# Sliding windows on one core: channel halves on partition halves, and output rows of 16 KB

## The chip, the cores and the metric

The kernel runs on one core of one Trainium2 chip. The metric is device time in microseconds for one execution, as the median of several.

## The reference

The input x holds 16 images of 64 channels, 64 x 64 float32 values each (16.8 MB). Windows of 8 x 8 are cut with a stride of 4 in both directions, 15 x 15 of them, and all are written out (59.0 MB). No arithmetic is done on the values.

```
n_h = (h - window_size) // stride + 1          # 15
n_w = (w - window_size) // stride + 1          # 15
result = np.zeros((batch, n_h, n_w, c, window_size, window_size), dtype=np.float32)
for i in range(n_h):
    for j in range(n_w):
        result[:, i, j] = x[:, :, i*stride : i*stride + window_size, j*stride : j*stride + window_size]
```

For one image and one window (i, j) the output is one contiguous run of 64 x 8 x 8 values, 16 KB.

## The kernel before

**Layout.** The whole input stays in SBUF in the tile L: 128 partitions, each with 32 channels of 16 image rows of 64 values (128 KB). A partition is an image (16), a channel half (2) and a quarter of the image's height (4), in this order, so that partition p is 8 x image + 4 x half + quarter. Within a quarter there are four window rows, numbered by the slot s = 0 to 3. Slot 3 needs the first four image rows of the next quarter, which lie on the next partition; the last quarter has no slot 3.

**Loads (L52).** Sixteen DMAs of 1 MB, eight issued from SP and eight from ACT, each with 32 partitions and 8 channels in runs of 4 KB.

**Index tiles (L62 to L78).** POOL writes the partition number, and DVE makes from it the output row at which each partition's store begins. In idx_last and idx_hlast the last quarter's rows are put out of range, and the scatter skips them.

**A window (L112 to L125).** One pass of the function window makes column j and slot s for all images and quarters at once, in a buffer of the tiles G. For slots 0 to 2 it is one ACT copy (L112). For slot 3 it is a DVE copy of the upper four rows (L114) and a DVE shuffle that brings the lower four from the next partition (L115). Then POOL issues an indirect DMA (L125), called scatter here, which writes one row of 8 KB for each partition, since a partition has half the channels. There are nine buffers of 1 MB. A copy into a buffer waits until the store that read it last has landed.

**Order.** For the first 8 windows the first 16 channels of each half are done first, with rows of 4 KB, because the load brings these channels earlier. The other halves of these windows alternate with whole windows, two and two. The last two windows are stored by seven plain DMAs from SP (L119), each for one quarter. Column by column, slots 0 to 3 follow each other. The engines' instructions are put in order by the framework, which also sets the waits; SP, ACT and POOL each have a DMA queue of their own, and all three use the same 16 DMA engines.

Of the kernel before, what the change touches and what calls it, by code (L numbers as in the profile page):

```python
# [1 line left out]

# [4 lines left out]


@with_exitstack  # L10
def kernel(
    ctx: ExitStack,
    tc: tile.TileContext,
    x: bass.AP,
    window_size: int,
    stride: int,
    out: bass.AP,
):
    nc = tc.nc
    P = nc.NUM_PARTITIONS  # L20

    B, C, H, W = x.shape
    Bo, NH, NW, Co, WSo, WSo2 = out.shape
    WS = int(window_size)
    ST = int(stride)
    assert Bo == B and Co == C and WSo == WS and WSo2 == WS

    f32 = mybir.dt.float32
    i32 = mybir.dt.int32
    ALU = mybir.AluOpType  # L30
    HQ = 4
    CH = P // (B * HQ)
    CL = C // CH
    RB = H // HQ
    NSLOT = RB // ST
    NWIN = NH * NW
    CFREE = CL * WS * WS
    assert HQ == 4 and CH == 2 and WS == 2 * ST

    lpool = ctx.enter_context(tc.tile_pool(name="lpool", bufs=1))  # L40
    ipool = ctx.enter_context(tc.tile_pool(name="ipool", bufs=1))
    gpool = ctx.enter_context(tc.tile_pool(name="gpool", bufs=1))


    L = lpool.tile([P, CL, RB, W], f32)
    x_v = x.rearrange("b (ch cl) (hq r) w -> hq (b ch) cl (r w)", ch=CH, hq=HQ)
    NCH = 4
    cw = CL // NCH

    for k in (2, 0, 1, 3):  # L50
        for q in range(HQ):
            (nc.sync, nc.scalar)[q % 2].dma_start(  # L52
                out=L[q::HQ, k * cw : (k + 1) * cw, :, :],
                in_=x_v[q, :, k * cw : (k + 1) * cw, :],
            )


    def itile(name):
        return ipool.tile([P, 1], i32, name=name)

    pi, tb, tq, tc_, idx, idx_last = (itile(n) for n in ("pi", "tb", "tq", "tc", "idx", "idx_last"))
    nc.gpsimd.iota(pi[:, :], pattern=[[0, 1]], base=0, channel_multiplier=1)  # L62
    nc.vector.tensor_scalar(out=tb[:, :], in0=pi[:, :], scalar1=3, scalar2=None, op0=ALU.logical_shift_right)  # L63
    nc.vector.tensor_scalar(out=tc_[:, :], in0=pi[:, :], scalar1=2, scalar2=1, op0=ALU.logical_shift_right, op1=ALU.bitwise_and)  # L64
    nc.vector.tensor_scalar(out=tq[:, :], in0=pi[:, :], scalar1=HQ - 1, scalar2=None, op0=ALU.bitwise_and)  # L65
    nc.vector.tensor_scalar(out=tb[:, :], in0=tb[:, :], scalar1=float(NWIN * CH), scalar2=None, op0=ALU.mult)  # L66
    nc.vector.tensor_tensor(out=tb[:, :], in0=tb[:, :], in1=tc_[:, :], op=ALU.add)  # L67
    nc.vector.tensor_scalar(out=tc_[:, :], in0=tq[:, :], scalar1=float(NSLOT * NW * CH), scalar2=None, op0=ALU.mult)  # L68
    nc.vector.tensor_tensor(out=idx[:, :], in0=tb[:, :], in1=tc_[:, :], op=ALU.add)  # L69

    nc.vector.tensor_scalar(out=tq[:, :], in0=tq[:, :], scalar1=float(HQ - 1), scalar2=float(2 * B * NWIN * CH), op0=ALU.is_equal, op1=ALU.mult)  # L71
    nc.vector.tensor_tensor(out=idx_last[:, :], in0=idx[:, :], in1=tq[:, :], op=ALU.add)  # L72


    HCL = CL // 2
    idx_h, idx_hlast = itile("idx_h"), itile("idx_hlast")
    for d, e in ((idx_h, idx), (idx_hlast, idx_last)):
        nc.vector.tensor_scalar(out=d[:, :], in0=e[:, :], scalar1=2.0, scalar2=None, op0=ALU.mult)  # L78
    o_v = out.rearrange("b i j (ch cl) r w -> (b i j ch) (cl r w)", ch=CH)
    o_h = out.rearrange("b i j (ch cl) r w -> (b i j ch) (cl r w)", ch=2 * CH)  # L80
    nxt = [min(p + 1, 31) for p in range(32)]

    order = [(j, s) for j in range(NW) for s in range(NSLOT)]


    TAIL, BACK = 2, 3
    o_q = out.rearrange("b i j (ch cl) r w -> i j b ch (cl r w)", ch=CH)

    def free(st):
        tc.declare_no_dep(st.ins, group="stores", reason="each store writes rows of its own")  # L90
        tc.add_to_no_dep_group("stores", st.ins)


    UNITS = 18
    G = [gpool.tile([P, 2 * HCL, WS, WS], f32, name=f"G{n}") for n in range(UNITS // 2)]
    at = 0

    def window(j, s, half):
        nonlocal at
        cols = slice(j * ST, j * ST + WS)  # L100
        last = s == NSLOT - 1
        if half is None:
            n, c0 = 2, 0
            at += at % 2
        else:
            n, c0 = 1, half * HCL
        u = at % UNITS
        at += n
        cs = slice(c0, c0 + n * HCL)
        g = G[u // 2][:, u % 2 * HCL : (u % 2 + n) * HCL, :, :]  # L110
        if not last:
            nc.scalar.copy(out=g, in_=L[:, cs, s * ST : s * ST + WS, cols])  # L112
        else:
            nc.vector.tensor_copy(out=g[:, :, 0:ST, :], in_=L[:, cs, s * ST : RB, cols])  # L114
            nc.vector.stream_shuffle(out=g[:, :, ST:WS, :], in_=L[:, cs, 0:ST, cols], mask=nxt)  # L115
        if (j, s) in order[-TAIL:]:
            g_q = g.rearrange("(m q) c r w -> q m (c r w)", q=HQ)
            for q in range(HQ - 1 if last else HQ):
                free(nc.sync.dma_start(out=o_q[q * NSLOT + s, j], in_=g_q[q]))  # L119
            return  # L120
        if half is None:
            o, ix = o_v, (idx_last if last else idx)
        else:
            o, ix = o_h, (idx_hlast if last else idx_h)
        st = nc.gpsimd.indirect_dma_start(  # L125
            out=o,
            out_offset=bass.IndirectOffsetOnAxis(ap=ix[:, 0:1], axis=0),
            in_=g.rearrange("p c r w -> p (c r w)"),
            in_offset=None,
            element_offset=(s * NW + j) * CH * CFREE + (half or 0) * HCL * WS * WS,  # L130
            bounds_check=B * NWIN * CH * (1 if half is None else 2) - 1,
            oob_is_err=False,
        )
        free(st)

    EARLY = 8
    for j, s in order[:EARLY]:
        window(j, s, 0)
    late = list(order[:EARLY])
    rest = list(order[EARLY:])  # L140
    while late:
        for w in late[:2]:
            window(*w, 1)
        for w in rest[:2]:
            window(*w, None)
        late, rest = late[2:], rest[2:]
    for w in rest[:-TAIL]:
        window(*w, None)
    at -= 2 * BACK
    for w in rest[-TAIL:]:  # L150
        window(*w, None)


# [1 line left out]
_INS = ['x', 'window_size', 'stride']  # L155
_OUTS = [((16, 15, 15, 64, 8, 8), 'float32')]

_NUMBERS = {'window_size': 8, 'stride': 4}


# [26 lines left out]
```

## Time and profile before

| what | value |
|---|---|
| median of 11 runs | 193.7 us (192.97 to 194.13) |
| profiled execution | 193.53 us, span 191.8 us |
| DVE busy | 30.2 us, 16% of the span |
| ACT busy | 86.2 us, 45% |
| POOL busy | 64.4 us, 34% |
| DMA | 75.80 MB, 395 GB/s on average |

Busy times are sums over the span of the profiled execution. POOL's busy time is nearly all from issuing scatters, 0.97 us each; the bytes move later, on the DMA engines. In a row of waits the numbers are the sum in us, how often, and the longest. In a group of instructions they are the busy time, the mean in ns, and the idle time of the engine just before, with what ended it. The 40 slices of the page are 4.8 us long each.

### The profile page before, as it was taken

The page shows a single profiled execution, that of the slowest core. Times are in us where ns is not written, and L with a number is a line of the kernel's source. Part 1 is how long each engine was busy: PE and PEld are TensorE (multiplying, and loading weights), DVE is VectorE, ACT ScalarE, POOL GpSimd, SP SyncE. Part 2 cuts the span into 40 slices and gives each one's busy share as a digit, 9 for nine tenths or more (in the row PEclk, how much of TensorE's full clock was granted, in tenths as well). Part 3 has the DMA queues.
Part 4 walks back from the last instruction along what each step waited for, and adds up shares of the span by engine and source line. Part 5 has one row for each costly group of instructions (what it writes and reads, how often), then busy time and mean ns, then how long its engine had stood idle before and what let it go on. Part 6 is the DMA issues. An engine that isn't in the chain of part 4 may idle for free.

```text
span 191.8 us, 458 instructions
## 1 busy us (share of the span) xinstructions
DVE 30.2 (16%) x62; ACT 86.2 (45%) x52; POOL 64.4 (34%) x71
## 2 busy tenths in 40 slices
DVE  2000000402322121211203120303030303000030
ACT  0000000494999646565655656474747373300300
POOL 0000000177877763543434344444444444400000
DMA  5999999999999999999999999999999999999785
GB/s 173 422 412 410 408 410 410 410 410 418 420 430 416 424 420 407 414 415 417 408 419 417 415 403 408 414 410 408 410 405 408 412 407 412 405 410 427 309 272 185
DMA packets 14196, 75.80 MB, mean 395 GB/s; under 512 B 1936, under 2 KB 1936, under 8 KB 7952
## 3 DMA queue, kind: packets, MB, share of 16 engines
q0 software_dynamic: 9504, 57.15, 73.1%
q1 hardware_dynamic: 2512, 10.22, 13.8%
q10 hardware_dynamic: 2176, 8.39, 11.1%
q14 instruction: 4, 0.03, 0.0%
HBM read 16.78 MB, written 62.65 MB: 414 GB/s over the span
## 4 chain that ended last, share of the span: by engine, by line
DMA 66%; issue 26%; POOL 3%; DVE 1%; POOLq 0%; DVEq 0%; PEldq 0%
DMA out_dram<-G,idx 57%; DMA out_dram<-G,idx_last 5%; DMA out_dram<-G,idx_h 4%; POOL out_dram L125 3%; DVE G L115 1%; DVE G L114 0%; POOLq L125 0%; POOL pi L62 0%; DVEq L114 0%; PEldq L182 0%
## 5 line engine op out<-in xcount | busy, mean ns | idle before, releaser
L112 ACT COPY G<-L 128x2048 f32<-128x2048 f32 (+1 forms) x51 | 84.9, 1696 | 59.3 <-DMA out_dram<-G,idx_last 25.0
L125 POOL DMA_INDIRECT out_dram<-G,idx x38 | 36.8, 969 | 49.6 <-DMA out_dram<-G,idx 46.4
L114 DVE COPY G<-L 128x1024 f32<-128x1024 f32 (+1 forms) x17 | 10.9, 638 | 152.9 <-DMA out_dram<-G,idx 88.5
L115 DVE STREAM_SHUFFLE G<-L 128x1024 f32<-128x1024 f32 (+1 forms) x17 | 19.5, 1146 | 0.0
L112 ACT ACT_TABLE_LOAD x1 | 1.3, 1283 | 36.2 <-DMA L<-in_x_dram 36.2
L125 POOL DMA_INDIRECT out_dram<-G,idx_hlast x4 | 4.0, 1004 | 37.6 <-DVE G L115 36.7
L125 POOL DMA_INDIRECT out_dram<-G,idx_last x12 | 11.6, 963 | 11.7 <-DVE G L115 7.8
L125 POOL DMA_INDIRECT out_dram<-G,idx_h x12 | 11.7, 975 | 3.7 <-issue 2.4
L63 DVE TENSOR_SCALAR tb<-pi 128x1 int32<-128x1 int32 x1 | 0.2, 153 | 1.0 <-POOL pi L62 1.0
L62 POOL IOTA pi<- 128x1 int32 x1 | 0.1, 121 | 0.4 <-PEq L182 0.4
L115 DVE LOAD_MASK_SELECT G<-L x17 | 0.2, 13 | 0.0
L168 POOL MEMSET const-float32-0.0<- 128x1 f32 x1 | 0.1, 99 | 0.2 <-issue 0.2
L69 DVE CUSTOM_DVE_ANT_0 idx<-tb,tc 128x2 uint16<-128x2 uint16 x1 | 0.2, 160 | 0.0
L67 DVE CUSTOM_DVE_ANT_0 tb<-tb,tc 128x2 uint16<-128x2 uint16 x1 | 0.2, 159 | 0.0
L78 DVE TENSOR_SCALAR idx_hlast<-idx_last 128x1 int32<-128x1 int32 x1 | 0.2, 155 | 0.0
L68 DVE TENSOR_SCALAR tc<-tq 128x1 int32<-128x1 int32 x1 | 0.2, 154 | 0.0
L78 DVE TENSOR_SCALAR idx_h<-idx 128x1 int32<-128x1 int32 x1 | 0.2, 154 | 0.0
L72 DVE CUSTOM_DVE_ANT_0 idx_last<-idx,tq 128x2 uint16<-128x2 uint16 x1 | 0.2, 153 | 0.0
L66 DVE TENSOR_SCALAR tb<-tb 128x1 int32<-128x1 int32 x1 | 0.1, 148 | 0.0
L71 DVE TENSOR_SCALAR tq<-tq 128x1 int32<-128x1 int32 x1 | 0.1, 147 | 0.0
L64 DVE TENSOR_SCALAR tc<-pi 128x1 int32<-128x1 int32 x1 | 0.1, 144 | 0.0
L65 DVE TENSOR_SCALAR tq<-pi 128x1 int32<-128x1 int32 x1 | 0.1, 143 | 0.0
(3 smaller groups left out, 0.3 us busy)
## 6 DMA issues: line engine op xcount, KB each, us to landing
L<-in_x_dram ACTq DMA_DIRECT2D x8, 1024.0 KB, 19.8
L<-in_x_dram SPq DMA_DIRECT2D x8, 1024.0 KB, 20.1
out_dram<-G SPq DMA_DIRECT2D x7, 256.0 KB, 4.2
out_dram<-G,idx POOLq DMA_INDIRECT x38, 18.7
out_dram<-G,idx_h POOLq DMA_INDIRECT x12, 7.0
out_dram<-G,idx_last POOLq DMA_INDIRECT x12, 18.8
out_dram<-G,idx_hlast POOLq DMA_INDIRECT x4, 8.0
```

Of the source, the lines that this page charges most:

```text
L62: nc.gpsimd.iota(pi[:, :], pattern=[[0, 1]], base=0, channel_multiplier=1)
L63: nc.vector.tensor_scalar(out=tb[:, :], in0=pi[:, :], scalar1=3, scalar2=None, op0=ALU.logical_shift_right)
L64: nc.vector.tensor_scalar(out=tc_[:, :], in0=pi[:, :], scalar1=2, scalar2=1, op0=ALU.logical_shift_right, op1=ALU.bitwise_and)
L67: nc.vector.tensor_tensor(out=tb[:, :], in0=tb[:, :], in1=tc_[:, :], op=ALU.add)
L68: nc.vector.tensor_scalar(out=tc_[:, :], in0=tq[:, :], scalar1=float(NSLOT * NW * CH), scalar2=None, op0=ALU.mult)
L69: nc.vector.tensor_tensor(out=idx[:, :], in0=tb[:, :], in1=tc_[:, :], op=ALU.add)
L72: nc.vector.tensor_tensor(out=idx_last[:, :], in0=idx[:, :], in1=tq[:, :], op=ALU.add)
L78: nc.vector.tensor_scalar(out=d[:, :], in0=e[:, :], scalar1=2.0, scalar2=None, op0=ALU.mult)
L112: nc.scalar.copy(out=g, in_=L[:, cs, s * ST : s * ST + WS, cols])
L114: nc.vector.tensor_copy(out=g[:, :, 0:ST, :], in_=L[:, cs, s * ST : RB, cols])
L115: nc.vector.stream_shuffle(out=g[:, :, ST:WS, :], in_=L[:, cs, 0:ST, cols], mask=nxt)
L125: st = nc.gpsimd.indirect_dma_start(out=o, out_offset=bass.IndirectOffsetOnAxis(ap=ix[:, 0:1], axis=0), in_=g.rearrange("p c r w -> p (c r ...
```

## The change

A partition now is a channel half (2), an image (16) and a quarter (4), in this order, so that partitions 0 to 63 hold channels 0 to 31 and partitions 64 to 127 hold channels 32 to 63. A buffer of G is 128 partitions with all 64 channels, 16 KB each, 2 MB together, and there are four. One buffer holds two slots: partitions 0 to 63 one, partitions 64 to 127 the other. Since the channels of a window lie on both halves of L, each half of a buffer is filled by two copies (by two copies and two shuffles for slot 3): one from its own partitions, one from the other 64.

The 24 loads take 8 partitions each. The images come in two groups of eight (y = 0, 1). For each group and quarter SP loads 28 channels of half 0, and POOL the other 4 channels of half 0 and then all 32 of half 1. ACT issues no loads. The index tiles are made ahead of the loads, by 21 DVE instructions in place of 11.

For the first three columns, slots 0 and 1 are done by image group, six units of 1 MB. In their scatters the rows of the other group are skipped; the buffer partitions that these skipped rows would read are filled with zeros by DVE first, eight fills. After that come 27 units of two slots each. Slots 0 and 1 take ACT for the copies on the same partitions and DVE for the shifted ones. Slots 2 and 3 take ACT for both copies of slot 2 and DVE for slot 3; which half of the buffer holds slot 3 alternates with the column. The last unit is slots 0 and 1 of the last column, stored by eight DMAs from SP, each with 16 rows of 16 KB.

The core of the diff:

```
-    HQ = 4
-    CH = P // (B * HQ)
+    CH = 2
+    HQ = P // (B * CH)
...
-    for k in (2, 0, 1, 3):
-        for q in range(HQ):
-            (nc.sync, nc.scalar)[q % 2].dma_start(
-                out=L[q::HQ, k * cw : (k + 1) * cw, :, :],
-                in_=x_v[q, :, k * cw : (k + 1) * cw, :],
-            )
+    x_v = x.rearrange("(y b) (ch cl) (hq r) w -> ch y hq b cl (r w)", y=NY, ch=CH, hq=HQ)
+    SMALL = 4
+    def load(eng, ch, y, q, c0, c1):
+        p0 = ch * HP + y * QP + q
+        eng.dma_start(out=L[p0 : p0 + QP - HQ + 1 : HQ, c0:c1, :, :], in_=x_v[ch, y, q, :, c0:c1, :])
...
+    for y in range(NY):
+        for q in range(HQ):
+            load(nc.sync, 0, y, q, SMALL, CL)
+            load(nc.gpsimd, 0, y, q, 0, SMALL)
+            load(nc.gpsimd, 1, y, q, 0, CL)
...
+    NG = 4
+    G = [gpool.tile([P, C, WS, WS], f32, name=f"G{n}") for n in range(NG)]
...
+    def fill(g, half, s, j, lo, n, copies):
+        d = slice(half * HP + lo, half * HP + lo + n)
+        cols = slice(j * ST, j * ST + WS)
+        for ch in (half, 1 - half):
+            f = slice(ch * HP + lo, ch * HP + lo + n)
+            cs = slice(ch * CL, (ch + 1) * CL)
+            copy = copies[ch != half]
+            if s < NSLOT - 1:
+                copy(out=g[d, cs, :, :], in_=L[f, :, s * ST : s * ST + WS, cols])
+            else:
+                copy(out=g[d, cs, 0:ST, :], in_=L[f, :, s * ST : RB, cols])
+                nc.vector.stream_shuffle(out=g[d, cs, ST:WS, :], in_=L[f, :, 0:ST, cols], mask=nxt)
...
+    EARLY = 3
+    for t in range(NG):
+        for half in range(CH):
+            p0 = half * HP + (QP if t < EARLY else 0)
+            nc.vector.memset(G[t][p0 : p0 + QP, :, :, :], 0.0)
+    t = 0
+    for y in range(NY):
+        for j in range(EARLY):
+            for half in range(CH):
+                copies = (dve, dve) if y and half and j == 1 else (act, dve)
+                fill(G[t % NG], half, half, j, y * QP, QP, copies)
+            scatter(G[t % NG], (idx_y0, idx_y1)[y], j, 0)
+            t += 1
...
+    units = [(j, s) for j in range(NW) for s in (0, 2) if s or j >= EARLY]
+    units.append(units.pop(-2))
+    for j, s in units:
+        g = G[t % NG]
+        t += 1
+        if s == 0:
+            for half in range(CH):
+                fill(g, half, s + half, j, 0, HP, (act, dve))
+            if (j, s) != units[-1]:
+                scatter(g, idx, j, s)
+                continue
+            g_q = g.rearrange("(ch b q) c r w -> ch q b (c r w)", ch=CH, q=HQ)
+            for q in range(HQ):
+                for half in range(CH):
+                    free(nc.sync.dma_start(out=o_q[q * NSLOT + s + half, j], in_=g_q[half, q]))
+        else:
+            turn = j % 2
+            fill(g, turn, s, j, 0, HP, (act, act))
+            fill(g, 1 - turn, s + 1, j, 0, HP, (dve, dve))
+            scatter(g, (idx_hi, idx_lo)[turn], j, s)
```

## The prediction

> **What bounds the kernel now.** I read the page's slices first, then its queue table, then the waits, then the groups kept apart by shape, and last the packet and landing records behind the DMA rows. The slices and the queues:
>
> ```profile
> DMA  5999999999999999999999999999999999999785
> GB/s 173 422 412 410 408 410 410 410 410 418 420 430 416 424 420 407 414 415 417 408 419 417 415 403 408 414 410 408 410 405 408 412 407 412 405 410 427 309 272 185
> DMA packets 14196, 75.80 MB, mean 395 GB/s; under 512 B 1936, under 2 KB 1936, under 8 KB 7952
> ...
> q0 software_dynamic: 9504, 57.15, 73.1%
> q1 hardware_dynamic: 2512, 10.22, 13.8%
> q10 hardware_dynamic: 2176, 8.39, 11.1%
> ```
>
> The 16 DMA engines are busy from the second slice to the 37th, at 403 to 430 GB/s; only the start and the last three slices (309, 272, 185) are below. The bytes, 16.8 MB in and 59.0 MB out, don't change. The waits agree:
>
> ```profile
> DVE G L114 <- DMA out_dram<-G,idx: 88.5, 10, 21.7
> POOL out_dram L125 <- DMA out_dram<-G,idx: 48.0, 30, 2.3
> ...
> ACT G L112 <- DMA out_dram<-G,idx_last: 25.0, 5, 14.8
> ACT G L112 <- DMA out_dram<-G,idx: 17.2, 20, 3.4
> ```
>
> ACT, DVE and POOL all wait for stores to land, so copies are free as long as stores stay queued. The packet records price the engines: a 4 KB packet usually takes 159 ns, an 8 KB one 309, and starts 3 ns before its predecessor ends, so 156 and 306 ns apart. By that line a 16 KB packet costs 606 ns, against 612 for two of 8 KB. The landing records have 16 entries for each DMA, one an engine, and show that the engines don't run alike: the 12th of 66 scatters has its last entry at 60.9 us, the 66th its first at 179.9 and its last at 185.5. The 54 between them give each engine 360 rows of 8 KB (36 whole scatters of 8, 12 of 6) and 44 of 4 KB: 110.2 + 6.9, and 0.6 for skipped rows and semaphores, 117.7 us. The slowest engine took 124.5, so 6.8 us (5.8%) were stalls; the fastest had 1.6. The slowest never starves and sets the end: 60.9 + 117.7 + 6.8, then 14 tail rows of 306 ns (4.3) and 1.2 us of their contention make 190.9; the last landing is at 190.8, the span 191.8, the execution 193.53, near the median of 193.7. So from the last landing to the time reported is 2.7 us.
>
> The copies, by shape:
>
> ```profile
> L112 ACT COPY G<-L 128x2048 f32<-128x2048 f32 x39 | 73.8, 1897 | 56.9 <-DMA out_dram<-G,idx_last 25.0 <-DMA out_dram<-G,idx 17.2 <-DVE G L115 13.3
> L115 DVE STREAM_SHUFFLE G<-L 128x1024 f32<-128x1024 f32 x13 | 16.6, 1278 | 0.0
> L114 DVE COPY G<-L 128x1024 f32<-128x1024 f32 x13 | 9.2, 705 | 106.1 <-DMA out_dram<-G,idx 88.5 <-DMA out_dram<-G,idx_h 9.6 <-ACT G L112 7.9
> L114 DVE COPY G<-L 128x512 f32<-128x512 f32 x4 | 1.7, 423 | 46.8 <-DMA L<-in_x_dram 41.3 <-DMA out_dram<-G,idx_h 5.5
> ```
>
> An ACT copy of 2048 elements a partition takes 1.90 us. DVE's went from 423 to 705 ns for 512 more elements, so 2048 make 1.27 us. Fewer partitions at the same elements should save nothing.
>
> [...] The tail stores of before took 396 ns on average instead of 309 for 8 KB, many about 626[...]. [...]
>
> ```profile
> 60.78 1.07 POOL L125 DMA_INDIRECT out_dram<-G,idx  x1 [0.30 <-ACT G L112]
> 61.04 0.69 DVE L114 COPY G<-L 128x1024 f32<-128x1024 f32 x1 [3.85 <-DMA out_dram<-G,idx]
> ```
>
> A copy wholly inside a scatter's issue made it 1.07 instead of 0.96 us.
>
> **The loads.** The first SP load should arrive as now (issue 0.7 us, first packet 2.2 us). ACT's eight issues go to POOL, which first makes the index tile (until 0.95 us), then a small load, then the first big one of channel half 1. No direct POOL DMA is in the trace; nearest is DMA_INDIRECT at 0.97 us for 128 rows. A big load has 256 packets, so I put its issue between 1 and 2 us and its first data between 3.2 and 5; I take 4.0[...]. [...]each engine gets 256 packets of 4 KB: 256 x 162 ns (mean of SP's queue) = 41.5 us, until 45.5. POOL's 16 issues, at most 32 us, lie under them and precede every scatter.
>
> **DVE before the first store.** Now 11 index operations run from 1.0 to 2.35 us, 0.124 us each; 21 take 2.6, until 3.6. Then come 8 zero fills of 32 x 4096. DVE has no such row. [...] Bounds: DVE copy pace gives 2.4 us each (19 in all), shuffle pace 5.1 (41). These fills now lie under the loads, but the cross copies behind them don't entirely: DVE needs 13 copies for the six early units, 16.5 us, to 55.3; then the first unit with s = 2 needs two copies and two shuffles, 3.97 us, to 59.3. ACT, with two copies for each unit except one, also reaches 59.3 after the second loads. Issue (0.96) and an estimated 1 us to first data: 61.2. The engines have 45.5 us of start and loads, then six units of 4 rows x 606 ns, 14.5 us: they could go on at 60.0. So 1.2 us is uncovered. The buffers that units 4 to 6 take again land near 48, 51 and 54, before DVE reaches them (49, 53, 55), so they add nothing; with the chain shorter they would be late next. Fills at copy pace would remove it (–1.2); shuffle pace would add 6. If partition-shifted copies take the shuffle's 2.5 us instead of 1.27, the chain grows by 16; if they go like the others, by nothing, which I take.
>
> **The long middle.** Each pair of units takes ACT 4 x 1.90 = 7.6 us and DVE 2 x 1.27 + 3.97 = 6.5, for 15 rows an engine, 9.1 us. Both hide. A freed G needs about 4 us of filling, 2 of issue and latency, while three units (some 14 us) are queued; that cover is used up only if the engines spread by more than 8 us (5 now). Waiting behind it would be POOL's next scatter and then every engine. An engine has 3600/16 = 225 rows of 16 KB, 24 of them early[...]. Before had 117.7 + 4.3 = 122.0 left at 60.9: so the late start and the DVE chain have used up what longer packets save (195 x 6 ns, and 18 ns for each of 30 rows now sent as four 4 KB packets: 1.7 us). Skipped rows fall on one half at a time, but alternate, 106 against 104 rows.
>
> **Stalls.** Between 60 and 80 us the mean 4 KB packet was 3 ns over its usual time, the 8 KB one 7: by bytes rather than by packets. I take 5.8% of 122.4 = 7.1 us. By packet it would be 6.8 x 202/404 = 3.4. Lower yet isn't excluded: from 50 to 60 us there was none.
>
> **The tail.** The last unit is stored from SP, 8 DMAs of 16 rows of one half[...]. It goes out beside queued scatters, so no refill gap follows; this doesn't help the slowest engine, which had none. Before lost 28% on its tail rows; of 8 x 606 ns that is 1.4. Bounds: 0 and 4.8.
>
> Sum: 61.2 + 122.4 + 7.1 + 1.4 = 192.1 for the last landing, plus 2.7: **194.8 us**, 1.3 over the profiled execution and 1.1 over the median.
>
> **Rivals.** *Stalls go by packet* or vanish with whole rows: 61.2 + 122.4 + 3.4 + 0 + 2.7 = 189.7, up to 192.5 with the tail's and some of the stalls. For it: 50 to 60 us without stalls; against it: the 3 and 7 ns. It decides once stalls fall below about 5.5 us. *The early chain is longer*: [...]shifted copies or fills at the slow pace, 3 to 8 us more: 197 to 203. Against it: 0.1 us in the rows above. *The loads pile up*: [...]77.8 us, 36 more: about 226. *Nothing net*: the pieces cancel, 193.7, as they nearly do in my sum.
>
> **The numbers.** About 0.2% is what a measurement of this kernel tells from no change. My case: 0.50 (slower 0.38, same 0.06, faster 0.06). Fewer stalls: 0.22, faster. Longer chain: 0.18, slower. Piled loads: 0.06, slower. Nothing net: 0.04 (same 0.03, faster 0.01). Together faster 0.29, same 0.09, slower 0.62. My case's own range is 193 to 197; 190 to 200 reaches into fewer stalls and most of the longer chain.
>
> **What would show it.** Right: 16 KB packets of about 609 ns; two load groups ending near 44 and 46 us; [...]first scatter issued near 41; slices at 405 to 412 GB/s from 65 us; DVE as the last release before the scatters up to 61 us. Wrong: slices of 425 or more in the middle (fewer stalls), a dip between 45 and 65 us (longer chain), half the GB/s during loads (piled loads), tail packets near 1,200 ns throughout.

## The result, and the profile after

The changed kernel takes 196.7 us (median of 8 runs, 196.52 to 197.07) against 193.7 (31 runs, 192.82 to 194.36): a ratio of 1.0159, 95% interval 1.0142 to 1.0176, so **3.0 us slower**. The forecast was 1.1 slower; 196.7 lies inside its range. The profiled execution took 196.96 us, its span is 195.2.

The slices, the packets and the queues of the changed kernel, in the page's order:

```profile
DMA  2999999999989999999999999999999999999983
GB/s 80 321 401 401 400 400 399 398 401 404 420 328 413 396 416 406 423 420 428 423 423 421 413 420 413 423 426 430 426 420 416 426 430 403 410 425 420 322 269 121
DMA packets 11588, 75.81 MB, mean 388 GB/s; under 512 B 3888, under 2 KB 3888, under 8 KB 7984
...
q0 software_dynamic: 9472, 66.34, 83.1%
q1 hardware_dynamic: 2112, 9.44, 13.6%
```

Slices are now 4.9 us long. The first two read 80 and 321 (before: 173 and 422), the load slices 398 to 404 (408 to 412), the twelfth falls to 328, and from the 17th on most lie between 413 and 430, above before's 403 to 420. So there is a loss at the start, one near 56 us, and a gain in the middle. Packet counts tell something else: packets under 512 bytes went from 1936 to 3888. The records show why: for each 4 KB packet that POOL loads with 8 partitions there is one of 4 bytes, which takes 9 ns.

To price these parts I read from the packet records when a given number of megabytes had moved, in both kernels:

| moved | before, us | after, us | lag |
|---|---|---|---|
| 2 MB | 7.6 | 10.0 | +2.4 |
| 10 MB | 27.1 | 29.9 | +2.8 |
| 16.78 MB (the size of the input) | 43.6 | 47.2 | +3.6 |
| 26 MB | 65.5 | 70.7 | +5.2 |
| 40 MB | 99.4 | 104.0 | +4.6 |
| 60 MB | 148.2 | 151.5 | +3.3 |
| 68 MB | 167.8 | 170.5 | +2.7 |
| 75.75 MB | 190.2 | 193.6 | +3.4 |

**Four terms**: +3.6 us during the loads, two thirds of it in the first 10 us; +1.6 while the first units are stored; -2.5 in the middle; +0.7 at the end. The sum, +3.4, is the difference of the two profiled executions (196.96 - 193.53). Busy times by stretch, first after (columns: from and to, length, busy us and instructions of DVE, ACT and POOL, TensorE clock, DMA share, GB/s):

```profile
2.40:5.00 2.60, 2.60 (x1) 0.00 (x0) 2.60 (x5) 1.00 0.47 154
5.00:10.00 5.00, 4.00 (x7) 0.00 (x0) 2.06 (x4) 1.00 0.97 327
54.00:58.00 4.00, 3.91 (x6) 3.95 (x3) 2.65 (x3) 1.00 0.78 316
62.00:64.00 2.00, 1.97 (x4) 1.98 (x2) 0.72 (x1) 1.00 0.74 311
75.00:100.00 25.00, 17.67 (x25) 23.46 (x13) 7.30 (x6) 1.00 1.01 420
185.00:190.00 5.00, 0.00 (x0) 0.00 (x0) 0.00 (x0) 1.00 0.82 262
```

then the same first stretches and the middle one of before:

```profile
2.40:5.00 2.60, 0.00 (x0) 0.00 (x0) 0.00 (x0) 1.00 0.96 345
5.00:10.00 5.00, 0.00 (x0) 0.00 (x0) 0.00 (x0) 1.00 1.02 419
...
75.00:100.00 25.00, 3.78 (x6) 15.18 (x8) 10.59 (x11) 1.00 1.01 414
```

Until 5.0 us half of the DMA time is unused (share 0.47 against 0.96). At 54 and at 62 us DVE and ACT are busy without a pause (3.91 and 3.95 of 4.00) while the DMA engines idle a quarter of the time: there the copies set the pace, on both engines (at 54 us together with POOL's slower issue, see e6). From 75 us on the DMA share is 1.01 in both kernels, with 4.7 times DVE's work and 1.5 times ACT's hidden.

The waits and the groups by shape, beside those shown of before:

```profile
POOL out_dram L119 <- ACT G L139: 50.4, 18, 3.9
ACT L139 <- DMA L<-in_x_dram: 29.8, 1, 29.8
POOL out_dram L119 <- DVE G L142: 26.0, 7, 4.6
...
POOL out_dram L119 <- DVE G L139: 12.3, 2, 8.6
...
ACT G L139 <- DMA out_dram<-G,idx: 10.1, 9, 1.5
```

```profile
L139 ACT COPY G<-L 64x2048 f32<-64x2048 f32 (+1 forms) x65 | 122.2, 1896 | 23.9 <-DMA out_dram<-G,idx 10.1
L139 DVE COPY G<-L 64x2048 f32<-64x2048 f32 (+1 forms) x37 | 45.2, 1232 | 16.9 <-DMA out_dram<-G,idx 11.5
L142 DVE STREAM_SHUFFLE G<-L 64x1024 f32<-64x1024 f32 x30 | 38.3, 1278 | 0.0
L153 DVE MEMSET G<- 32x4096 f32 x8 | 27.8, 3472 | 7.9 <-issue 6.2
```

Before, ACT, DVE and POOL waited for stores to land. Now POOL's waits are for ACT's and DVE's copies (50.4, 26.0 and 12.3 us), and no single wait of ACT or DVE for a store exceeds 2.5 us. The slack has shrunk; in the middle it is still enough. A copy between partition halves costs what another costs: ACT's 65 copies, of both kinds, took 1.89 to 1.90 us each, with 32 or 64 partitions (before, with 128: 1.90), and DVE's 30 of 1024 elements, of both kinds too, 0.68 to 0.73; DVE's of 2048 elements took 1.23 on average.

### The profile page after: what moved, and what is told of

The parts are those of the page before. It is cut to its first block, busy times and chain, and to the rows that moved or that the text cites. A ratio compares the mean times of both kernels' runs of the same rounds, so it can differ in the third digit from the quotient of the medians.

```text
span 195.2 us, 485 instructions
## 1 busy us (share of the span) xinstructions
DVE 132.4 (68%) x156; ACT 123.5 (63%) x66; POOL 51.6 (26%) x53
## 3 DMA queue, kind: packets, MB, share of 16 engines
HBM read 16.78 MB, written 69.21 MB: 441 GB/s over the span
## 4 chain that ended last, share of the span: by engine, by line
DMA 66%; DVE 17%; issue 3%; POOL 2%; ACTq 1%; ACT 1%; DVEq 0%; PEldq 0%
DMA out_dram<-G,idx 21%; DMA L<-in_x_dram 18%; DMA out_dram<-G,idx_hi 15%; DMA out_dram<-G,idx_lo 12%; DVE G L139 8%; DVE G L142 6%; DVE G L141 3%; POOL L L57 2%; ACTq L216 1%; ACT G L139 1%; DVEq L139 0%; POOL pi L68 0%; DVEq L141 0%; PEldq L216 0%; ACTq L139 0%
## 5 line engine op out<-in xcount | busy, mean ns | idle before, releaser
L139 ACT COPY G<-L 64x2048 f32<-64x2048 f32 (+1 forms) x65 | 122.2, 1896 | 23.9 <-DMA out_dram<-G,idx 10.1
L139 DVE COPY G<-L 64x2048 f32<-64x2048 f32 (+1 forms) x37 | 45.2, 1232 | 16.9 <-DMA out_dram<-G,idx 11.5
L142 DVE STREAM_SHUFFLE G<-L 64x1024 f32<-64x1024 f32 x30 | 38.3, 1278 | 0.0
L153 DVE MEMSET G<- 32x4096 f32 x8 | 27.8, 3472 | 7.9 <-issue 6.2
L141 DVE COPY G<-L 64x1024 f32<-64x1024 f32 x30 | 20.7, 690 | 18.2 <-DMA out_dram<-G,idx_hi 10.2
L119 POOL DMA_INDIRECT out_dram<-G,idx_hi x8 | 12.2, 1530 | 30.3 <-DVE G L142 17.9
L119 POOL DMA_INDIRECT out_dram<-G,idx x11 | 11.8, 1070 | 30.7 <-ACT G L139 26.2
L57 POOL DMA_DIRECT2D L<-in_x_dram x16 | 9.8, 626 | 25.1 <-DMA L<-in_x_dram 24.6
L119 POOL DMA_INDIRECT out_dram<-G,idx_lo x7 | 8.6, 1235 | 20.2 <-ACT G L139 11.1
L119 POOL DMA_INDIRECT out_dram<-G,idx_y x6 | 8.7, 1458 | 14.2 <-DVE G L139 12.3
```

The source lines that it names most:

```text
L57: eng.dma_start(out=L[p0 : p0 + QP - HQ + 1 : HQ, c0:c1, :, :], in_=x_v[ch, y, q, :, c0:c1, :])
L119: st = nc.gpsimd.indirect_dma_start(out=o_v, out_offset=bass.IndirectOffsetOnAxis(ap=ix[:, 0:1], axis=0), in_=g.rearrange("p c r w -> p (c ...
L139: copy(out=g[d, cs, :, :], in_=L[f, :, s * ST : s * ST + WS, cols])
L141: copy(out=g[d, cs, 0:ST, :], in_=L[f, :, s * ST : RB, cols])
L142: nc.vector.stream_shuffle(out=g[d, cs, ST:WS, :], in_=L[f, :, 0:ST, cols], mask=nxt)
L153: nc.vector.memset(G[t][p0 : p0 + QP, :, :, :], 0.0)
```

## The experiments

Each kernel is the changed one, or the one before, with one edit. Ratios are against the kernel before, measured beside it; the changed kernel's is 1.0159.

**e1: the zero fills on ACT** instead of DVE.

```
-            nc.vector.memset(G[t][p0 : p0 + QP, :, :, :], 0.0)
+            nc.scalar.copy(out=G[t][p0 : p0 + QP], in_=<zero tile [P, WS], broadcast>)
```

> The changed kernel with its eight zero fills on ACT (reading a small zero tile) instead of DVE. Theory A, [...]first POOL load data near 3.5 us instead of 5.2, loads over near 46 instead of 48.2, DVE's first copies near 35 instead of 38.9, the time 1.5 to 3 us shorter, 193.7 to 195.2. Theory B, loads issued by POOL are slow by themselves whatever DVE does: first data stays at 5 us or later, loads still end near 48, the time within 0.5 us of 196.7.

196.94 us, ratio 1.0162 (1.0138 to 1.0186): nothing. POOL's first load data came at 4.95 us instead of 5.18, the loads' last landing at 48.05 instead of 48.16. DVE began its copies at 29.7 us and the first scatter was issued 5.8 us sooner, at 38.69, yet every later mark of the table is within 0.3 us of the changed kernel's until 70 MB. Its start is as poor without DVE fills:

```profile
2.40:5.00 2.60, 1.48 (x10) 2.60 (x1) 2.60 (x5) 1.00 0.51 158
```

So the fills neither hold up POOL's loads nor cost time where they lie. Earlier scatters bought nothing, since the loads filled the DMA engines then (share 1.03 from 10 to 44 us).

**e4: POOL's big load ahead of its small one**, to see whether their order decides which loads share the DMA engines.

```
-            load(nc.gpsimd, 0, y, q, 0, SMALL)
             load(nc.gpsimd, 1, y, q, 0, CL)
+            load(nc.gpsimd, 0, y, q, 0, SMALL)
```

> The changed kernel with POOL's big load ahead of its small one in each group. [...]the big loads now fall on the engines that SP's loads use, these engines get 480 of the 512 packets, the load phase runs at some 215 GB/s and lasts 75 to 85 us, the time 220 to 235 us. If the engines follow from the partitions: nothing changes, 196 to 198 us.

229.73 us in its one run. Its loads run at half the rate for 50 us:

```profile
GB/s 109 259 211 224 208 226 210 226 208 228 207 372 278 264 214 283 414 388 411 420 437 413 417 417 421 431 414 417 417 437 420 420 414 440 417 413 414 362 288 135
```

An order of two instructions decides 33 us. From 10 us on half of the DMA time is unused, where the changed kernel (second line) has none to spare:

```profile
10.00:50.00 40.00, 23.03 (x22) 0.00 (x0) 3.62 (x6) 1.00 0.55 216
10.00:44.00 34.00, 28.06 (x27) 12.27 (x7) 4.27 (x7) 1.00 1.04 400
```

The landing records show how narrow a load is: an SP load of 8 partitions in the changed kernel has 8 entries when it lands, a POOL load of 8 partitions 16, mostly in two groups of eight (the first's at 3.2 to 3.3 and at 8.2 to 9.1 us), and a load of 32 partitions in the kernel before 16 in one group. A share of 0.55 fits big loads that fall on the eight engines SP's loads use. The packet records don't name the engine, so which loads met on which engines was not shown. The changed kernel leaves no DMA time unused from 10 us on, so the loss at the start isn't a pile-up.

**b1: in the kernel before, ACT's eight loads issued by POOL**, after its index instruction; still 32 partitions each.

```
-            (nc.sync, nc.scalar)[q % 2].dma_start(
+            (nc.sync, nc.gpsimd)[q % 2].dma_start(   # and placed after the index tiles
```

> The kernel before with the eight loads that ACT issues issued by POOL instead, and the index tiles made ahead of them; each load still has 32 partitions. Theory A, what POOL loads cost in the changed kernel is half of the engines lying idle until the first POOL data at 5 us, plus some 9 ns for an extra small packet beside each 4 KB: here SP's loads fill all 16 engines from 2.3 us, so only 128 small packets an engine remain, 0.5 to 1.3 us more, 194.3 to 195.1. Theory B, a POOL load is slow in itself: 2 us or more, 195.7 and up.

194.49 us, ratio 1.005 (1.003 to 1.007), 0.9 us more than before, of which +0.2 us at 16.78 MB; the rest comes while stores run, and its cause is open. POOL's first data came as late as ever, at 5.24 us, but the DMA engines didn't notice:

```profile
2.40:5.00 2.60, 0.00 (x0) 0.00 (x0) 2.60 (x5) 1.00 0.93 337
5.00:10.00 5.00, 0.00 (x0) 0.00 (x0) 1.16 (x3) 1.00 1.02 410
```

SP's loads of 32 partitions alone take 0.93 of the 16 engines' time until POOL's arrive. In the changed kernel SP's loads of 8 partitions take 0.47, and the rest stays unused until POOL's come. So it is the pair, late POOL data and narrow loads, that costs the 2.4 us at 2 MB.

**b3: in the kernel before, the changed kernel's 8-partition loads** from SP and POOL, in two steps of 16 channels because the order of its windows needs that (48 loads instead of 24).

```
+        eng.dma_start(out=L[HQ * n0 + q : HQ * n0 + q + 29 : HQ, c0:c1, :, :], in_=x_v[q, n0 : n0 + 8, c0:c1, :])
...
+                load(nc.sync, 8 * y, q, c0 + SMALL, c0 + HCL)
+                load(nc.gpsimd, 8 * y, q, c0, c0 + SMALL)
+                load(nc.gpsimd, 16 + 8 * y, q, c0, c0 + HCL)
```

> The kernel before with the load scheme of the changed one alone: loads of 8 partitions, SP for 32 of the 64 partition pairs' first half with a small POOL load beside each, POOL for the other half, in two steps of 16 channels; layout, copies, rows and stores stay as before. Theory A, the load scheme itself costs what the two traces differ by at the end of the loads (3.6 us): [...]loads over near 47 instead of 43.6, and the loss stays to the end: 196.5 to 198. Theory B, the loss belongs to the new layout and its fills: loads over near 44 to 45, the time 193.5 to 195.

202.12 us, ratio 1.0445 (1.0419 to 1.0472), more than either theory gave. It reproduces the start (165 GB/s from 2.4 to 5.0 us, +3.0 us at 10 MB), but then loses 4.3 us more by 16.78 MB, most of it from 24 us on:

```profile
10.00:42.00 32.00, 2.04 (x6) 6.79 (x7) 10.48 (x19) 1.00 1.01 373
```

The 4 KB packets of POOL's loads grow longer there, 201 ns on average from 25 to 30 us where the changed kernel has 164. The number of POOL loads is doubled in this experiment alone, which may be the reason, but isn't shown: POOL waits for earlier loads to land for 25.2 us in all, hardly more than in the changed kernel (24.6). It confirms the place of the start's loss, not its size in the end.

**e7: an extra load from SP for half 1**, to occupy the other engines until POOL's data come.

```
+    nc.sync.dma_start(out=L[HP : P - HQ + 1 : HQ, 0:FIRST, :, :], in_=x_f[1, 0, :, 0:FIRST, :])   # FIRST = 6, 16 partitions
-            load(nc.gpsimd, 1, y, q, 0, CL)
+            load(nc.gpsimd, 1, y, q, 0 if q else FIRST, CL)
```

> The changed kernel with one more SP load in front: 6 channels of half 1's first quarter, 16 partitions, on all 16 engines; POOL's two loads of that quarter are shorter by these channels. Theory A, [...]loads end near 46.5 instead of 48.2, the time 0.8 to 1.8 us shorter, 194.9 to 195.9. Theory B, the load phase is limited by what the POOL loads do between 5 and 45 us: loads still end near 48, the time within 0.4 us of 196.7.

197.85 us, ratio 1.0221 (1.0196 to 1.0245): 1.1 us slower than the changed kernel, where both theories had it faster or equal. The engines were busy (share 0.81 until 5.0 us) but moved little:

```profile
2.40:5.00 2.60, 2.60 (x1) 0.00 (x0) 2.60 (x5) 1.00 0.81 205
5.00:10.00 5.00, 4.00 (x7) 0.00 (x0) 2.02 (x4) 1.00 0.97 308
```

SP's 4 KB packets took 282 to 358 ns on average between 3.5 and 5.0 us instead of 159, POOL's first few 1158 in the half microsecond after. The extra load goes to partitions 64 to 127 alone, as POOL's big loads do; why packets take longer then was not shown. Filling the hole in this way gained 0.1 us at 2 MB and delayed what followed: the last load landed at 48.90 us instead of 48.16, and the mark of 26 MB came 0.7 us later.

**e3: another order of units**, slots 0 and 1 alternating with 2 and 3 from the start, so that DVE's dearer units (3.97 us) don't follow each other.

```
+    for n in range(NW - 4):
+        units += [(EARLY + n, 0), (n, 2)]
```

> The changed kernel with the order of the whole units changed: slots 0 and 1 of columns 3 to 13 alternate with slots 2 and 3 of columns 0 to 10, so that after the six early units DVE has 2.5 us of copies in every other unit instead of 4 us in three in a row. Theory A, DVE's chain is the bound from 48 to 75 us: the dips between 54 and 68 us shrink to one, the time 0.5 to 1.5 us shorter. Theory B, [...]the dips stay and the time is within 0.4 us of 196.7.

196.77 us, ratio 1.0149 (1.0124 to 1.0173): no change, and the dips stay (303 GB/s from 54 to 58 us, 287 from 62 to 64). ACT needs 3.8 us for every unit whatever its slots, and was as far behind as DVE. The time is the one that theory B gave, but the run doesn't single out a cause: beside the copies, POOL's issues were slow here too (2.35, 1.86 and 1.71 us).

**e6: the fifth and sixth early units not filled**, which takes 5 copies from DVE and 3 from ACT.

```
-                fill(G[t % NG], half, half, j, y * QP, QP, copies)
+                if y == 0 or j == 0:
+                    fill(G[t % NG], half, half, j, y * QP, QP, copies)
```

> The changed kernel without the fills of the fifth and sixth early unit (five DVE and three ACT copies left out, so these two units store old data). Theory A, after the loads land at 48 us ACT and DVE can't make early units as fast as the engines store them, and this is the 1.6 us lost between 17 and 26 MB: the dips between 54 and 68 us go, the time 1 to 1.8 us shorter, 194.9 to 195.7. Theory B, the dips come from POOL's issue alone: within 0.4 us of 196.7.

196.03 us, ratio 1.0122 (1.0099 to 1.0145), between the two theories. The dips are gone:

```profile
54.00:58.00 4.00, 2.62 (x6) 2.62 (x2) 1.19 (x2) 1.00 1.03 418
62.00:64.00 2.00, 1.97 (x4) 1.98 (x2) 0.18 (x1) 1.00 1.04 430
```

and the table's marks come 1.4 us sooner from 26 MB on, but only 0.7 us of it reaches the time. So the copies, with POOL's slower issue beside them, make the second term (+1.6). The changed kernel's timeline (shown further down) tells the two apart in part. The scatter before the dip at 62 us waited 2.89 us for ACT's copies and was issued in the usual 0.96: there it is the copies alone. The one before the dip at 54 us waited 3.64 us for copies and then took 2.44 to issue, so that POOL's issue has a share. Where the other 0.7 us went the semaphore records show: SP's last row landed 1.6 us sooner (192.66 against 194.26), but POOL's last scatter only 0.8 (191.41 against 192.20), and POOL's closing event came at 193.47, after SP's end; e2 and d1 are about this wait.

**e5: whole units stored as two scatters of 8 KB rows** instead of one of 16 KB.

```
-                scatter(g, idx, j, s)
+                scatter2(g, idx2, j, s)      # for h in range(2): rows of CFREE // 2, index x 2, + h * CFREE // 2
```

> The changed kernel with each whole unit but the last written by two scatters of 8 KB rows instead of one of 16 KB rows; copies, buffers and order stay. Theory A, rows of 16 KB are what makes the middle faster than before (2.5 us from 26 to 68 MB): the time grows by 1.2 us from packets alone (190 rows, 6 ns each) to 3 us with stalls, 197.9 to 199.7. Theory B, the middle is faster because the engines are held together by the four buffers and the row length does nothing: within 0.5 us of 196.7.

204.4 us, ratio 1.0557 (1.0533 to 1.058), 7.7 us more than the changed kernel and more than theory A gave. From 26 to 68 MB it took 103.2 us, where the changed kernel took 99.9 and the kernel before 102.3:

```profile
75.00:100.00 25.00, 17.68 (x24) 23.77 (x13) 16.05 (x13) 1.00 1.01 405
125.00:150.00 25.00, 17.08 (x23) 19.78 (x11) 14.94 (x11) 1.00 1.01 408
```

An 8 KB packet usually takes 309 ns and here took 324 on average, 15 over; the changed kernel's 16 KB packets usually take 611 and took 626, also 15 over. Between these two kernels **stalls**, the time over the usual, **go by packet**: half the size, twice the stalls. That the number of scatters doubled too wasn't separated from the size. The two profiled executions differ by 7.1 us (204.06 against 196.96): 3.3 come in the middle and 1.0 after 68 MB, to a last packet 4.15 us later (198.07 against 193.92), and 2.9 follow the last landing, since POOL is released at 201.54, 3.1 us after it.

**e2: the last unit scattered by POOL** too, instead of eight DMAs from SP.

```
-            if (j, s) != units[-1]:
-                scatter(g, idx, j, s)
-                continue
+            scatter(g, idx, j, s)
+            continue
```

> The changed kernel with its last unit stored by one scatter of 128 rows from POOL, not by eight DMAs from SP of 16 rows of one half. Theory A, the tail loses some 2.5 us[...]: 16 KB packets stay near 620 ns to the end, the time 1.5 to 2.5 us shorter, 194.2 to 195.2. Theory B, the slowest engine sets the end and has the same bytes either way: the time within 0.5 us of 196.7, with low slices at the end all the same.

195.41 us, ratio 1.0086 (1.0065 to 1.0107), 1.3 us less, just short of theory A's range. The engines stay full to 185 us and are done before 191:

```profile
180.00:185.00 5.00, 0.00 (x0) 0.00 (x0) 0.00 (x0) 1.00 1.01 426
185.00:190.00 5.00, 0.00 (x0) 0.00 (x0) 0.00 (x0) 1.00 0.64 272
190.00:194.00 4.00, 0.00 (x0) 0.00 (x0) 0.00 (x0) 1.00 0.00 0
```

It had moved 75.75 MB at 190.0 us, the kernel before at 190.2, and yet e2 is 1.6 us slower than before. The difference lies after the last landing (190.78): POOL's last semaphore event before the end comes 2.1 us later, at 192.88. Before, POOL's scatters had landed by 185.46, and SP's tail, to 190.78, covered that wait. In the changed kernel the two ends fall together: POOL's last scatter landed at 192.20 and its closing DRAIN instruction ended at 194.21, SP's at 194.41. An earlier end of SP alone can gain 0.2 us at most: in e1 and e3 SP's last row landed 0.6 and 0.7 us sooner (193.62, 193.58), and POOL's closing event, at 194.56 and 194.41, kept the time where it was.

**d1: in the kernel before, the last two windows scattered by POOL** as well, to put that to the test where nothing else is changed.

```
-        if (j, s) in order[-TAIL:]:
+        if False:
```

> The kernel before with its last two windows stored by POOL's scatters as all others, and no reuse of late buffers for them. Theory A, POOL is released 2.1 us after its last scatter lands, as in the run with the changed kernel's tail on POOL: the last landing comes 1 to 3 us earlier than 190.8, but the end follows 2.8 us after it instead of 1.0, the time 192.5 to 195. Theory B, the end follows the landing by 1 us whoever stored: 190.5 to 192.5.

194.51 us, ratio 1.0056 (1.0034 to 1.0078). Its last packet ended 1.8 us *sooner* than before (188.70 against 190.47), its time is 1.1 us *longer*:

```profile
185.00:190.00 5.00, 0.00 (x0) 0.00 (x0) 0.00 (x0) 1.00 0.34 141
190.00:194.00 4.00, 0.00 (x0) 0.00 (x0) 0.00 (x0) 1.00 0.00 0
```

The span lasts until 192.6; POOL was released at 191.89, 2.9 us after its last landing at 189.02. So the wait after a last scatter is real in both kernels.

**e9: e2 and e6 together.**

> The changed kernel with the tail on POOL and without the fills of the fifth and sixth early unit (these two units store old data). If the two losses are separate they add: 196.7 less 1.3 less 0.7, 194.7, and if the whole 1.4 us that the early fills cost comes through to the end, 194.0. If one covers the other: 195.2 to 195.6.

194.96 us, ratio 1.0076 (1.0054 to 1.0098): 1.75 us less than the changed kernel, against 1.3 + 0.7 = 2.0. That would be nearly additive, but by the ratios, each to the kernel before measured beside it, e9 can't be told from e2 alone (1.0086, 1.0065 to 1.0107), so that adding up isn't shown. It is still slower than before: what is left is mainly the loads' 3.6 us less the middle's 2.5, with POOL's release.

**d2: in the kernel before, one tail window from SP instead of two**, to look for a balance of both ends.

```
-    TAIL, BACK = 2, 3
+    TAIL, BACK = 1, 2
```

> The kernel before with one window instead of two stored from SP, in the buffer of the scatter before the last. If POOL's release, some 3 us after its last scatter lands, is what SP's tail has to cover and no more, a shorter tail is enough: last landing near 190, the end near 191, the time 192.6 to 193.3. If the cover is too short, POOL's release ends the kernel: 193.5 to 194.5.

194.37 us, ratio 1.0044 (1.0028 to 1.006). The time lies where the second case put it, but not for its reason: the last scatter landed at 187.31 and POOL's DRAIN was over at 190.09, while SP's last row landed at 191.40, later than the 190 that was expected, and ended the kernel. The kernel before was better balanced. No version of this study beats it.

## Why the prediction was right or wrong

The direction was right and the forecast mechanism, a start that eats up what long packets save, was right in kind. The sum can be compared step by step, for the slowest engine, at the prediction's 202 rows of 606 ns (122.4 us): unit 7 is the first whole one; unit 8 lands 15 rows after it starts, unit 31 another 172 rows later, and 15 rows remain.

| step of the sum | predicted | measured | difference |
|---|---|---|---|
| 61.2, then 15 rows with stalls: unit 8 landed | 70.8 | 73.00 | +2.2 |
| 172 rows x 606 ns, with stalls: unit 31 landed | 110.3 | 109.4 | -0.9 |
| 15 rows and the tail | 11.0 | 11.8 | +0.8 |
| from there to the time reported | 2.7 | 2.7 | 0.0 |
| sum | 194.8 | 197.0 | +2.2 |

The middle's -0.9 and the tail's +0.8 cancel by luck.

**The failing step is "61.2"**, the start of the first whole unit, too early by some 2.5 us. Three of its terms were off. "I take 4.0" for POOL's first load data: 5.18, just past the upper bound of 5. "256 x 162 ns": POOL's packets took 168, SP's 170, so that the engines that wait for POOL ended at 5.18 + 256 x 0.168 = 48.2 and not at 45.5 (the last landing is at 48.16); 1.2 us is the late start and 1.5 the packets. The 162 came from a queue whose loads had 32 partitions; the loads of 8 have the 4-byte packets besides, which may be part of it; that wasn't tested. And DVE's chain was taken as running on from 38.8 (its 55.3 less 16.5 of copies). It did begin there, but stopped:

```profile
38.93 7.00 DVE L139 COPY G<-L 32x2048 f32<-32x2048 f32 x6 [0.21 <-issue]
44.53 1.53 POOL L119 DMA_INDIRECT out_dram<-G,idx_y  x1 [8.62 <-DVE G L139]
...
48.18 15.23 ACT L139 COPY G<-L 32x2048 f32<-32x2048 f32 x8 [6.12 <-issue]
48.23 8.86 DVE L139 COPY G<-L 32x2048 f32<-32x2048 f32 x7 [2.29 <-issue]
52.27 2.44 POOL L119 DMA_INDIRECT out_dram<-G,idx_y  x1 [3.64 <-DVE G L139]
55.35 1.86 POOL L119 DMA_INDIRECT out_dram<-G,idx_y  x1 [0.64 <-issue]
...
61.76 0.96 POOL L119 DMA_INDIRECT out_dram<-G,idx_hi  x1 [2.89 <-ACT G L139]
```

By this timeline ACT sat idle for 6.1 us and DVE for 2.3 until the second image group was in, at 48.2; both then work without a gap. The late loads thus delay the copies, and the copies the stores: the first whole unit's scatter was issued at 61.76 instead of about 59.3. "ACT also reaches 59.3" had named the second bound, and it is the one the trace puts last: from 48.18 on seven copies of 1.90 us end at 61.5. That another order for DVE changed nothing (e3) fits. The prediction gave the loads and DVE's copies a chain each, where in fact both engines' copies stand behind one event, the landing of the last loads.

**The first scatter** was put near 41 us and issued at 44.53, since the framework let DVE make the first half of three units before the second halves. e1 shows that this was harmless.

**The fills** were 3.47 us each, between the prediction's bounds of 2.4 and 5.1, with gaps of 0.9 and index instructions between, so that DVE's copies began at 38.9 against 38.8. The value it took for one fill rested on no trace; it was too long, and the gaps were left out: right in sum, by two errors that cancelled. Costing them at little was right (e1).

**POOL's issue beside copies.** The longer-chain rival stood against a row with 0.1 us. Two scatters among back-to-back DVE copies took 2.44 and 1.86 us to issue instead of 0.96; in e6 two with no DVE copy beside them, at 52.01 and 53.28 us, took 0.96 each. How a copy delays an issue was not shown. The delays' share of the +1.6 wasn't isolated: e6 removed both the copies and these delays.

**Stalls.** 5.8% was taken; the slowest engine had 109.4 - 104.2 = 5.2 us in 104.2, 5.0%. The size was nearly right. The reasoning, "by bytes rather than by packets", was not: e5 has them by packet, and the share came out near only because each packet stalls longer in this structure. An 8 KB packet stalls 15 ns on average in e5, in the kernel before 10; what raises it (more copying on DVE and ACT, other source partitions) wasn't tried. By e5 the middle's gain of 2.5 us is the 3.3 that 16 KB rows save less 0.9 that the rest of the new structure costs (103.2 us against 102.3); the 160 rows an engine of this stretch save at most 160 x 6 ns = 1.0 us by their usual time, so fewer stalls are the larger part of the 3.3. The forecast had 1.7 from longer packets over the whole remainder and nothing from stalls.

**The tail.** "It goes out beside queued scatters" held only in part:

```profile
175.24 14.60 SPq L179 DMA_DIRECT2D out_dram<-G  x8
```

SP issues from 175.24 us on, but its first row moves at 180.1, behind whole scatters (DMA share 1.03 from 175 to 180 us), and its rows take 917 ns on average for 16 KB where 611 is usual, 1295 at the 90th percentile. Why they take longer was not shown. Taking 1.4 us for that fell short by 0.8. The prediction lacked a term, POOL's release, which SP's tail had covered in the kernel before: in the changed kernel POOL's DRAIN ends 0.2 us before SP's, so that both set the end. e2, which ends both queues' stores sooner and pays POOL's release, gains 1.3 us.

**The rivals.** Piled loads exist and give 229.7 (e4), but only in the other order; the prediction's own terms for them, 194.8 and 36 more (77.8 for 480 packets of 162 ns, against 41.5), make nearer 230 than its "about 226". Stalls were fewer by 0.9 us, which is short of the half that this rival needed. Two signs of being wrong that the prediction had named did appear, a dip between 45 and 65 us and slices of 425 or more in the middle (7 of the 21 from the 17th on). The longer chain (197 to 203) is nearest to what happened, by another mechanism: late loads ahead of it rather than slow copies in it.

## What to carry to other kernels

Before narrowing a DMA to fewer partitions, count who feeds each DMA engine in the first microseconds: a queue whose data start late cost 0.2 us by the end of the loads while another covered all engines (b1), and 2.4 us at 2 MB where half of the engines' time had no other (share 0.47). When loads gate copies and copies gate stores, take the latest input as the start of each chain and don't let a chain run on from where its first part could begin. Look at when each queue's end is reported, not only at when its bytes land: leave the last stores to a queue whose end is quick (in the changed kernel SP's came 0.15 us after its last landing, POOL's 2.0), and weigh that against how long its rows wait behind what is already queued.

## What the runs showed of the hardware

- POOL's first 4 KB packet starts 3.7 us after its issue begins (1.48 to 5.18 us), with 8 or 32 partitions alike (5.24 in b1), and with the fills on ACT (4.95); only in e7 was it sooner, at 3.43. In the changed kernel POOL's queue ran 40 packets of 4 bytes at 2.86 us already, so the queue itself wasn't what began late. Why the data did is open.
- After a last scatter has landed, POOL is released 2.0 to 2.1 us later in the changed kernel, e1, e2, e3 and e6 (32 or 33 scatters), 2.7 to 2.9 in the kernel before, d1 and d2 (66 to 68), and 3.1 in e5 (58). Why it differs wasn't tried.
- In the changed kernel's loads by POOL there is a 4-byte packet of 9 ns for each 4 KB packet; in b1's loads of 32 partitions there is none.
- A load of 32 partitions has 16 landing entries in the kernel before, an SP load of 8 partitions 8 in the changed kernel, a POOL load of 8 partitions and an SP store of 16 rows 16, mostly in two groups of eight. From 3 to 5 us 8.2 packets of 4 KB were in flight on average in the changed kernel, all of them SP's, and 16.3 in the kernel before.
- In the changed kernel the eight zero fills of 32 x 4096 took DVE 3.47 us each.
- Mean stalls of about 15 ns a packet at 8 KB (e5) and at 16 KB (the changed kernel), with the same copies beside them.
